# The first weight tile of the second layer is split in the gate tile's room, and the list of layer 1 gets new numbers

## The chip, the cores and the metric

The kernel runs on one core of a Trainium2 chip. The core has a TensorE for matmuls (PE in the profile; its weight loads are PEld), a VectorE (DVE), a ScalarE (ACT), a GpSimd (POOL), and a SyncE (SP) that here does nothing but issue DMAs. The metric is the device time of one execution in microseconds.

## The reference

One inference step of a small two-layer trunk with a model width of 1024, over 128 prompt tokens and 512 sample tokens. Each layer is an RMS norm, a shift and scale from the conditioning, a branch, and a gated residual. Layer 0's branch is a Conformer convolution, layer 1's a bidirectional Mamba-2 scan. What matters here is layer 1, cut to its core:

```python
def ssd_branch(h, h0_f, h0_b, w_in, w_conv, b_conv, dt_bias_f, dt_bias_b, a_log_f, a_log_b, d_skip, norm_g, w_out):
    u = h @ w_in
    z, xbc, dt_raw = jnp.split(u, [SSD_INNER, SSD_INNER + XBC_DIM], axis=-1)
    xbc = jax.nn.silu(depthwise_conv(xbc, w_conv, b_conv))
    xs, bm, cm = jnp.split(xbc, [SSD_INNER, SSD_INNER + SSD_GROUPS * D_STATE], axis=-1)
    ...
    dt_f = jax.nn.softplus(dtr_f + dt_bias_f.astype(f32))
    ...
    y_f, s_f = ssd_scan(xs, dt_f, a_f, bm, cm, h0_f)
    y_b, s_b = ssd_scan(flip(xs), flip(dt_b), a_b, flip(bm), flip(cm), h0_b)
    y = y_f + flip(y_b) + d_skip.astype(f32)[:, None] * xs.astype(f32)
    y = y.reshape(b, l, SSD_INNER) * jax.nn.silu(z.astype(f32))
    y = rms_norm(...)
    return y.astype(h.dtype) @ w_out, s_f, s_b
```

The inner width is 2048, in 32 heads of 64 that form 4 groups; the scan runs in chunks of 128 tokens (one of the prompt, four of the sample) with a state of 128.

## The kernel before

**Tiles.** Activations lie feature-major: a tile has 128 features on the partitions and all 640 tokens on the free axis, worked in two halves of 320. The input of layer 1, h, is eight such tiles. A float32 product is made of three fp32r matmuls, from a high and a low part of each operand: high by high, low by high, high by low. A weight tile of 128x1024 is loaded by an SP DMA into `wf` (two buffers), cast by ACT into its high part `wh`, and DVE subtracts that from `wf` for the low part `wl`. `wh` and `wl` are rings of three buffers each, shared by both layers.

**Layer 1's projections.** Every weight tile gives one projection tile of 48 matmuls, 320 columns wide: 8 tiles of h, 3 products, 2 halves (`project`, whose matmuls stand at L1327). There are x tiles (four per group, `x03` is group 0's last), b and c tiles (one per group) and z tiles (the gates, four per group). dt and the first two x tiles (x00, x01) are multiplied already at the end of layer 0 (L1051); they lie in `first`. After the projections of a group come the convolution over tokens, the scan of its five chunks, the norm, and the products with the output weights (`o` items, L1580, and `last_products`, L1938, for the last group), whose sums are added into x. The last group's y passes the transposes `pty` (L1750) and a sum of squares `ssp` (L1861) on PE.

**The order.** Layer 1 is written as generators that hand their steps to a list scheduler, the class `Order`. Whenever an engine's step can begin, by the list's own clocks and rings of buffers, the step of the best priority (`PRIO1`) is issued, and the tiles are taken in the order of the string `PLAN1`. So a number in these tables moves instructions on all engines. The list's clocks are set at the seam by hand: `run.clock` says when PE, ACT, DVE, POOL, SP and the DMAs are free, `run.rings.update` when the rings' buffers are, and `start(first_steps(), ...)` when dt is there. On the chip, each instruction waits for what it needs by semaphores; the list only decides the order on each engine.

**The seam.** `first_steps` empties dt's bank into `room` in two times three steps (L2133, where the list may choose ACT or DVE, and L2142, always DVE); dt's bank and the banks of x00 and x01 are the ones that layer 1's first projections take. `first_x` empties those of x00 and x01 into `up` by `evacuate` (L1357, ACT or DVE). The first weight tile's split (`split`, the case `i == 0`) is made in two halves of 512 columns, L1284 on ACT and L1271 on DVE, so that the first matmuls can begin behind the first half; all other tiles are split at L1255 and L1264.

**The gate tile.** `zs` is a room for four tiles of 640 columns that holds the gates of a group of z tiles; there is one such buffer, and nothing uses it before the first z tile of group 0.

**The end.** PLAN1 ends, before, with `x30 o10 z22 o11 x31 z23 c3 z30 z31 z32 o20 z33 o21`: group 3's last x tile is x31.

Of the kernel before, what the change touches and what calls it, by code (L numbers as in the profile page):

```python
# [8 lines left out]
F32R = mybir.dt.float32r  # L9
# [4 lines left out]
P = 128  # L14
NT = 640
# [25 lines left out]
PRIO0 = {"warm": 9, "firsts": 7, "ada_chain": 5, "modulation0": 3, "sums0": 4, "square0": 7, "first_split": -7, "conv": 3, "after_a": -5, "after_g": -7, "init": -7, "late_taps": 1, "late_adds": 3, "seam": 2, "copied": -6, "after_z": -7, "weights": 7, "split": -4, "row": 5, "square": -2, "filler": 5, "blocks": -1, "add_sums": -2, "stats": -5, "means": -3, "normalise": -4, "gate_z": 6, "late_block": -5, "residual": -3, "half_residual": -1, "root": -1, "modulation": 5, "split_h": 0, "scales": 6}  # L41
PLAN0 = "a1 z0 g2 a2 g3 a3 g4 a4 g5 a5 g6 a6 g7 a7 g8 a8 g9 a9 g10 z1 z2 a10 z3 g11 a11 g12 a12 g13 a13 g14 z4 a14 g15 z5 z6 a15 z7 z8 z9 z10 z11 z12 z13 z14 z15"
NPOOL = (12, 6, 12, 6, 12, 11, 8, 10, 2, 8, 9, 8, 12, 4, 6, 8)
PRIO1 = {"first_x": -4, "first_half": -6, "dt_way": 0, "x_way": 1, "late_weights": 0, "lead": -4, "sq_way": -3, "add_way": 6, "squares": -5, "room": -4, "roots": 4, "turn_x": -5, "gate_rows": -2, "gate_loads": 5, "residual": 5, "last_products": -3, "last_residual": -6, "final": -2, "gained_half": -7, "low": 6, "x_after": -2, "filler": 7, "decay_half": -7, "decay_state": -2, "chain0": -3, "chain1": 5, "other_y": -3, "copy_y": 2, "split_y": -5, "groups": 4, "decays": -6, "norms": 5, "gate": 7, "products1": 3, "products0": -1, "residual0": -6, "final0": -6, "w_chain": 6, "time_steps": 5, "columns": -5, "logarithm": 4, "rows_out": 7, "ends_out": 4, "weights_out": 5, "first_steps": 5, "b_after": 0, "c_after": 0, "z_after": -6, "split": -6, "add_residual": 1, "out_weights": 0, "free_bc": 2, "final1": -2, "prompt": -1, "residual1": 3, "store": -5, "final_rest": 1}
PLAN1 = "x03 x02 c0 x10 b0 z00 c1 z01 x12 x13 x33 x22 z02 x11 b1 z03 x20 c2 x23 z10 z11 z12 z13 x21 x32 b2 o00 b3 o01 z20 z21 x30 o10 z22 o11 x31 z23 c3 z30 z31 z32 o20 z33 o21"
RB1 = {"xs": 3, "st": 6, "gf": 2, "gb": 1}
WARM0 = 6
DONE0 = []
# [3 lines left out]
def trunk(ctx: ExitStack, tc: tile.TileContext, a: dict):  # L52
    nc = tc.nc
    PSUM = bass.MemoryType.PSUM
    gp = ctx.enter_context(tc.tile_pool(name="gp", bufs=1))
# [191 lines left out]
    class Order:  # L247
# [112 lines left out]
    def get(name):  # L360
        return "get", name
# [23 lines left out]
    if True:  # L385
        run = Order(PRIO0)
        post, put, start = run.post, run.put, run.start
# [56 lines left out]
        wa0, w0, x_sq, psx = {}, {}, {}, []  # L444
# [154 lines left out]
    with tc.tile_pool(name="l0", bufs=1) as lp:  # L599
# [9 lines left out]
        for i in range(3):  # L609
            t = lp.tile([P, 2, 30], F32, name=f"eb{i}")  # L610
# [309 lines left out]
        yh, yl = [None] * 16, [None] * 16  # L920
# [261 lines left out]
    lp = l1_ctx.enter_context(tc.tile_pool(name="l1", bufs=1))  # L1182
    if True:
# [7 lines left out]
        up = []  # L1191
# [37 lines left out]
        run = Order(PRIO1)  # L1229
        post, put, start = run.post, run.put, run.start  # L1230

        for name, n in (("wf", 2), ("wh", 3), ("wl", 3), ("up", 0), ("bc", 2), ("Bt", 1), ("xt", 2), ("zs", 1), ("yh", 0), ("yl", 0), ("xw", 2), ("y", 1), ("y3", 0), ("yo", 2), ("tr", 1), ("b", 3), ("gt", 1), *RB1.items()):
            run.ring(name, n)
        run.rings["mm"] = []

# [9 lines left out]
        def w_load(i, src, g=None):  # L1245
            cell = {}

            def load():
                cell["wf"] = gp.tile([P, 1024], F32, tag="wf", bufs=2, name="wf")
                nc.sync.dma_start(out=cell["wf"], in_=src)  # L1250

            def high():
                cell["wh"] = gp.tile([P, 1024], F32R, tag="wh", bufs=3, name="wh")
                if g is None:
                    S.copy(out=cell["wh"], in_=cell["wf"])  # L1255
                else:
                    for z_, sn in gained(g, cell):
                        S.activation(out=cell["wh"][:, z_], in_=cell["wf"][:, z_], func=AF.Copy, scale=sn)

            def low(e_, n=0):  # L1260
                if n == 0:
                    cell["wl"] = gp.tile([P, 1024], F32R, tag="wl", bufs=3, name="wl")
                if g is None:
                    e_.tensor_sub(out=cell["wl"], in0=cell["wf"], in1=cell["wh"].bitcast(F32))  # L1264
                else:
                    (z_, sn), = gained(g, cell)[n : n + 1]
                    e_.scalar_tensor_tensor(out=cell["wl"][:, z_], in0=cell["wf"][:, z_], scalar=sn, in1=cell["wh"][:, z_].bitcast(F32), op0=ALU.mult, op1=ALU.subtract)

            def first_half(n, t):
                z_ = slice(n * 512, n * 512 + 512)  # L1270
                t = yield either((VL, 0.69, lambda: V.tensor_sub(out=cell["wl"][:, z_], in0=cell["wf"][:, z_], in1=cell["wh"][:, z_].bitcast(F32))), (PO, 1.25, lambda: G.tensor_sub(out=cell["wl"][:, z_], in0=cell["wf"][:, z_], in1=cell["wh"][:, z_].bitcast(F32))), bias=0.5)  # L1271
                if n:
                    put("wf", t)
                W[i] = cell["wh"], cell["wl"]
                post(("w", i, "b") if n else ("w", i), t)

            def split():
                if i == 0:
                    yield get("wh")
                    yield get("wl")  # L1280
                    cell["wh"] = gp.tile([P, 1024], F32R, tag="wh", bufs=3, name="wh")
                    cell["wl"] = gp.tile([P, 1024], F32R, tag="wl", bufs=3, name="wl")
                    for n in range(2):
                        t = yield op(ACT, 0.62, lambda: S.copy(out=cell["wh"][:, n * 512 : n * 512 + 512], in_=cell["wf"][:, n * 512 : n * 512 + 512]))  # L1284
                        start(first_half(n, t), t)
                    return
                yield get("wh")
                yield op(ACT, 1.05 if g is None else 1.24, high)
                yield get("wl")
                if g is None:  # L1290
                    t = yield either((VL, 1.22, lambda: low(V)), (PO, 2.41, lambda: low(G)), bias=PRIO1["low"])
                else:
                    yield op(VL, 0.77, lambda: low(V))
                    t = yield op(VL, 0.77, lambda: low(V, 1))
                put("wf", t)
                W[i] = cell["wh"], cell["wl"]
# [861 lines left out]

        with tc.manual_schedule():
            S.activation(out=an, in_=c("alog"), func=AF.Exp)  # L2160
# [146 lines left out]
```

## Time and profile before

| what | value |
|---|---|
| median of 3 runs | 1057.93 us (1057.34 to 1058.88) |
| profiled execution | 1056.0 us, its span 1054.2 us |
| granted TensorE clock | 0.997 |
| PE busy | 98% of the span, 7497 instructions |
| layer 1's first projection matmul | at 544.95 us |
| last x tile of group 3 ends on PE | at about 915.5 us |
| last matmul | begins just before 1046 us |

A row of the timeline gives the start in us, the busy time, engine, line, operation, and what is written from what; in brackets stands how long the engine had been idle and what released it. A row of a window gives the stretch and the busy time of PE, PEld, DVE, ACT and POOL. PE's busy time counts pipelined matmuls, so an idle gap is read from the times of the rows' starts.

### The profile page before, as it was taken

The page shows a single profiled execution, that of the slowest core. Times are in us where ns is not written, and L with a number is a line of the kernel's source. Part 1 is how long each engine was busy: PE and PEld are TensorE (multiplying, and loading weights), DVE is VectorE, ACT ScalarE, POOL GpSimd, SP SyncE. Part 2 cuts the span into 40 slices and gives each one's busy share as a digit, 9 for nine tenths or more (in the row PEclk, how much of TensorE's full clock was granted, in tenths as well). Part 3 has the DMA queues.
Part 4 walks back from the last instruction along what each step waited for, and adds up shares of the span by engine and source line. Part 5 has one row for each costly group of instructions (what it writes and reads, how often), then busy time and mean ns, then how long its engine had stood idle before and what let it go on. Part 6 is the DMA issues. An engine that isn't in the chain of part 4 may idle for free.

```text
span 1054.2 us, 19251 instructions
## 1 busy us (share of the span) xinstructions
PE 1030.5 (98%) x7497; PEld 945.9 (90%) x7497; DVE 814.8 (77%) x1219; ACT 670.5 (64%) x1115; POOL 475.8 (45%) x472
## 2 busy tenths in 40 slices
PE   6999999999999999999999999999999999999996
PEld 4999999999999999999989998899888878897865
DVE  3599999998997679202589858889598777896797
ACT  6468788778687578433477755588665455474534
POOL 0029989978596511111000046414544555426551
PEclk9999999999999999999999999999999999999998
DMA  9597888788856666777112252333424334323423
GB/s 355 205 269 196 195 210 202 180 212 215 186 123 143 136 143 149 150 155 165 61 58 85 83 160 91 110 115 107 131 83 120 117 101 130 113 98 104 126 81 100
DMA packets 64363, 151.82 MB, mean 144 GB/s; under 512 B 9472, under 2 KB 22416, under 8 KB 64272
## 3 DMA queue, kind: packets, MB, share of 16 engines
q1 hardware_dynamic: 54048, 118.87, 35.9%
q0 software_dynamic: 8640, 30.94, 17.4%
q8 instruction: 59, 0.97, 0.4%
q10 hardware_dynamic: 1584, 0.79, 0.3%
q14 instruction: 32, 0.26, 0.1%
HBM read 145.45 MB, written 5.12 MB: 143 GB/s over the span
## 4 chain that ended last, share of the span: by engine, by line
PE 86%; DVE 7%; ACT 2%; DMA 2%; issue 2%; SPq 0%; DVEq 0%; ACTq 0%
PE xs L1327 9%; PE pz L1327 8%; PE o L1580 6%; PE pst L1660 3%; PE po L1723 2%; PE C L1327 2%; PE B L1327 2%; PE py L1791 2%; PE o__4964 L158 1%; PE o__5264 L158 1%; PE o__5273 L158 1%; PE o__5251 L158 1%; PE o__5244 L158 1%; PE o__4954 L158 1%; PE xs L1051 1%
## 5 line engine op out<-in xcount | busy, mean ns | idle before, releaser
L815 DVE SCALAR_TENSOR_TENSOR cva<-v,cst,cva 128x550 f32<-128x550 f32 (+12 forms) x346 | 270.2, 823 | 11.2 <-ACT cva L807 6.1
L887 POOL TENSOR_TENSOR cv<-cv,tp 128x490 f32<-128x490 f32 (+5 forms) x134 | 172.5, 1287 | 8.5
L846 ACT ACTIVATE tp<-v,cst 128x490 f32<-128x490 f32 (+5 forms) x134 | 92.3, 717 | 35.9 <-POOL cv L887 35.5
L425 ACT CAST wh<-wf 128x1024 fp32r<-128x1024 f32 x63 | 66.0, 1047 | 63.9 <-PE o__5273 L158 30.0
L1327 PE MATMUL pz<-h_hi,wh 128*128 128x320 f32 x256 | 87.2, 341 | 0.0
L1327 PE MATMUL pz<-h_hi,wl 128*128 128x320 f32 x256 | 79.1, 309 | 0.0
L1327 PE MATMUL pz<-h_lo,wh 128*128 128x320 f32 x256 | 79.0, 309 | 0.0
L1327 PE MATMUL xs<-h_hi,wh 128*128 128x320 f32 x224 | 77.0, 344 | 1.9 <-DVE room L2142 1.9
L1327 PE MATMUL xs<-h_hi,wl 128*128 128x320 f32 x224 | 69.4, 310 | 0.1
L1327 PE MATMUL xs<-h_lo,wh 128*128 128x320 f32 x224 | 69.1, 309 | 0.0
L1373 DVE SCALAR_TENSOR_TENSOR xs<-up,cst,xs 128x642 f32<-128x642 f32 x64 | 64.8, 1013 | 3.2 <-ACT xs L1371 1.9
L1729 POOL TENSOR_TENSOR y<-y,yo 128x512 f32<-128x512 f32 x32 | 45.4, 1421 | 41.4 <-DVE yo L1727 41.4
L1255 ACT CAST wh<-wf 128x1024 fp32r<-128x1024 f32 x37 | 38.6, 1046 | 38.3 <-PE pz L1327 10.6
L435 ACT ACTIVATE wl<-wh 128x1024 fp32r<-128x1024 f32 x58 | 61.5, 1061 | 1.7
L436 POOL DMA_DIRECT2D wl<-w_in x43 | 37.4, 869 | 55.0 <-ACT wl L435 52.0
L1597 POOL TENSOR_TENSOR gb<-gb,cols 128x512 f32<-128x512 f32 x20 | 25.8, 1290 | 79.3 <-DMA gb<-acb 79.3
L1559 POOL TENSOR_TENSOR x<-x,tmp 128x512 f32<-128x512 f32 x30 | 45.5, 1520 | 34.5 <-DVE tmp L1555 34.4
L1264 DVE TENSOR_TENSOR wl<-wf,wh 128x1024 fp32r<-128x1024 f32 x37 | 48.5, 1315 | 14.6 <-ACT wh L1255 12.8
L1603 ACT ACTIVATE gf<-gf,cols 128x128 f32<-128x128 f32 x160 | 50.6, 391 | 10.4 <-DVE gf L1599 10.0
L436 POOL DMA_DIRECT2D wl<-w_out x15 | 12.9, 862 | 90.5 <-ACT wl L435 90.5
L1580 PE MATMUL o<-wh,yh 128*128 128x512 f32 x120 | 52.4, 436 | 0.4 <-DVE tmp L1555 0.4
L1327 PEld LDWEIGHTS pz<-h_hi,wh 128*128 128x128 f32 x256 | 48.2, 188 | 3.5 <-issue 3.4
(849 smaller groups left out, 3536.1 us busy)
## 6 DMA issues: line engine op xcount, KB each, us to landing
wf<-w_in SPq DMA_DIRECT2D x48, 512.0 KB, 3.7
wl<-w_in POOLq DMA_DIRECT2D x43, 512.0 KB, 6.4
wa<-w_ada SPq DMA_DIRECT2D x64, 256.0 KB, 5.9
wf<-w_out SPq DMA_DIRECT2D x32, 512.0 KB, 3.6
wf<-w_xbc SPq DMA_DIRECT2D x24, 512.0 KB, 3.6
gf<-acf SPq DMA_DIRECT2D x40, 256.0 KB, 4.0
wa<-w_ada SPq DMA_DIRECT2D x16, 512.0 KB, 10.8
wf<-w_z SPq DMA_DIRECT2D x16, 512.0 KB, 3.6
```

What stands on the lines that cost most here:

```text
L158: T.matmul(ps[:, b, at : at + t1 - t0], lhsT=w, rhs=h[:, t0:t1], start=first and n == 0, stop=last and n == 2)
L425: t = yield op(ACT, 1.05, lambda: S.copy(out=wh, in_=wf))
L435: yield op(ACT, 1.06, lambda: S.activation(out=wl, in_=wh.bitcast(F32), func=AF.Copy, scale=-1.0))
L436: t = yield op(PD, 0.7, lambda: G.dma_start(out=wl, in_=src, accum_op=ALU.add))
L815: t = yield op(VE, 0.24 + 0.01 * (hi - lo), lambda: V.scalar_tensor_tensor(out=rows64(accs[i], lo, hi), in0=rows64(vs[i], lo + d, hi + d), ...
L846: t = yield op(ACT, 0.72, lambda: S.activation(out=tp[:, :, 0 : hi - lo], in_=rows64(vs[i], lo + d, hi + d), func=AF.Copy, scale=w_dw(i, t ...
L887: t = yield op(PO, 1.3 + 0.019 * (hi - lo - 49), lambda: G.tensor_add(out=rows64(cv[i], lo, hi), in0=rows64(cv[i], lo, hi), in1=sgs["tp", ...
L1264: e_.tensor_sub(out=cell["wl"], in0=cell["wf"], in1=cell["wh"].bitcast(F32))
L1327: T.matmul(ps[:, b, at_ : at_ + t1 - t0], lhsT=w_, rhs=t_[:, t0:t1], start=k == 0 and n == 0, stop=k == nk - 1 and n == 2)
L1373: t = yield op(VL, 0.97, lambda: V.scalar_tensor_tensor(out=acc, in0=u[:, d : d + PW], scalar=c("w_c", j * 5 + d), in1=acc, op0=ALU.mult, ...
L1580: T.matmul(ps, lhsT=t_, rhs=w_, start=k == 0 and n == 0, stop=k == 3 and n == 2)
L1603: t = yield op(ACT, 0.39, lambda: S.activation(out=gv[:, h_, :], in_=gv[:, h_, :], func=AF.Exp, bias=cols1[ch][:, o8 + h_ : o8 + h_ + 1]), ...
```

## The change

Three things change, and all other code stays.

1. The first weight tile (item 0 of the list) takes the room of `zs`, as a tile called `w0`: its first 1024 columns are the high part, the next 1024 the low. It takes no buffer of the rings `wh` and `wl`; when its projection has been multiplied, `w_free` gives `zs` back.
2. The list's times at the seam: ACT's and DVE's clocks go from −2.0 to −3.0, the free times of `wh` and `wl` from −1.8, −0.9, 0.0 to −0.8, −0.4, 0.0, the start of `first_steps` from −1.8 to −0.8, of `first_x(0)` from −0.9 to −0.4.
3. All of `PRIO1` and `PLAN1` is new.

```diff
-PLAN1 = "x03 x02 c0 x10 b0 z00 c1 z01 x12 x13 x33 x22 z02 x11 b1 z03 x20 c2 x23 z10 z11 z12 z13 x21 x32 b2 o00 b3 o01 z20 z21 x30 o10 z22 o11 x31 z23 c3 z30 z31 z32 o20 z33 o21"
+PLAN1 = "b0 x12 z00 c0 x03 x02 x10 x33 z01 z02 x23 x13 z03 c1 x11 b1 z10 z11 z12 x20 x31 o00 x21 x22 z13 o01 z20 c2 b2 z21 x30 z22 z23 b3 o10 c3 o11 x32 z30 z31 z32 o20 z33 o21"
...
-        for name, n in (("wf", 2), ("wh", 3), ("wl", 3), ("up", 0), ("bc", 2), ("Bt", 1), ("xt", 2), ("zs", 1), ...
+        for name, n in (("wf", 2), ("wh", 3), ("wl", 3), ("up", 0), ("bc", 2), ("Bt", 1), ("xt", 2), ("zs", 0), ...
...
                 if i == 0:
-                    yield get("wh")
-                    yield get("wl")
-                    cell["wh"] = gp.tile([P, 1024], F32R, tag="wh", bufs=3, name="wh")
-                    cell["wl"] = gp.tile([P, 1024], F32R, tag="wl", bufs=3, name="wl")
+                    yield get("zs")
+                    room_ = lp.tile([P, 4, NT], F32R, tag="zs", bufs=1, name="w0").rearrange("p a b -> p (a b)")
+                    cell["wh"], cell["wl"] = room_[:, 0:1024], room_[:, 1024:2048]
...
         def w_free(i, t):
+            if i == 0:
+                put("zs", t)
+                return
             put("wh", t)
             put("wl", t)
...
-            run.clock = [0.0, -2.0, -2.0, -2.0, -9.0, -9.0]
+            run.clock = [0.0, -3.0, -3.0, -2.0, -9.0, -9.0]
...
-            run.rings.update(wf=[-9.0, -9.0], wh=[-1.8, -0.9, 0.0], wl=[-1.8, -0.9, 0.0])
+            run.rings.update(zs=[-9.0], wf=[-9.0, -9.0], wh=[-0.8, -0.4, 0.0], wl=[-0.8, -0.4, 0.0])
...
-            start(first_steps(), -1.8)
-            start(first_x(0), -0.9)
+            start(first_steps(), -0.8)
+            start(first_x(0), -0.4)
```

Line numbers behind `split` move by two at most: L1284 becomes L1283, L1327 becomes L1329, L1357 becomes L1359. In the new code the L2133 form is ACT's step for dt, and DVE's two are L2135 and L2144. The order of layer 0's instructions is the same on every engine.

ACT at the seam, from the first instruction of layer 1 (`an`) on. `up_6270` and `up_6274` are the copies of x00 and x01, `dt` is dt's bank; the names in brackets are the semaphores that the instruction waits for (DMAHW5 is the load of the weights). Before:

```order
L2160 ACTIVATE an<-cst 128x1 [waits DVE_49]
L1284 CAST wh<-wf 128x512 [waits DMAHW5_49,PE_49]
L1284 CAST wh<-wf 128x512
L1255 CAST wh<-wf 128x1024 [waits DMAHW6_49,PE_49]
L1357 COPY up_6270<-xs 128x128 [waits PE_49]
L1357 COPY up_6274<-xs 128x64
L1357 COPY up_6274<-xs 128x64 [waits PE_49]
L1357 COPY up_6270<-xs 128x512
```

and in the changed kernel:

```order
L2162 ACTIVATE an<-cst 128x1 [waits DVE_49]
L1283 CAST w_6300<-wf 128x512 [waits DMAHW5_49]
L1283 CAST w_6300<-wf 128x512
L1255 CAST wh<-wf 128x1024 [waits DMAHW6_49,PE_49]
L1359 COPY up_6270<-xs 128x128 [waits PE_49]
L2133 ACTIVATE room_6286<-dt,cst 32x128 [waits DVE_49,Pool_49]
L1359 COPY up_6270<-xs 128x512
L2133 ACTIVATE room_6286<-dt,cst 32x256
```

The first two casts no longer wait for PE, and two steps of dt have come over from DVE, one of them ahead of the second copy of x00.

DVE at the same place, from its first step of dt on; before:

```order
L2133 TENSOR_SCALAR room_6286<-dt,cst 32x128 [waits DMASW0_49,DMASW1_49,DVE_49,DMAHW6_49,PE_49,Pool_49]
L2133 TENSOR_SCALAR room_6286<-dt,cst 32x256
L2142 TENSOR_SCALAR room_6286<-dt,cst 32x256
L2133 TENSOR_SCALAR room_6286<-dt,cst 32x128
L2133 TENSOR_SCALAR room_6286<-dt,cst 32x256
L2142 TENSOR_SCALAR room_6286<-dt,cst 32x256
L1271 TENSOR_TENSOR wl<-wf,wh 128x512 [waits DMAHW5_49,Activation_49]
L1271 TENSOR_TENSOR wl<-wf,wh 128x512 [waits Activation_49]
L1264 TENSOR_TENSOR wl<-wf,wh 128x1024 [waits DMAHW6_49,PE_49,Activation_49]
```

and in the changed kernel:

```order
L2135 TENSOR_SCALAR room_6286<-dt,cst 32x128 [waits DMASW0_49,DMASW1_49,DVE_49,DMAHW6_49,PE_49,Pool_49]
L2135 TENSOR_SCALAR room_6286<-dt,cst 32x256
L2144 TENSOR_SCALAR room_6286<-dt,cst 32x256
L1271 TENSOR_TENSOR w_6300<-wf,w_6300 128x512 [waits DMAHW5_49,Activation_49]
L1271 TENSOR_TENSOR w_6300<-wf,w_6300 128x512 [waits Activation_49]
L1264 TENSOR_TENSOR wl<-wf,wh 128x1024 [waits DMAHW6_49,Activation_49]
L2144 TENSOR_SCALAR room_6286<-dt,cst 32x256 [waits Activation_49]
```

The split of the first tile now stands behind three steps of dt instead of six, and dt's last step behind the split of the second tile.

PE, from the last matmul of layer 0 on; before:

```order
L1051 MATMUL xs<-h_hi,wh 128x320
L1051 MATMUL xs<-h_lo,wh 128x320
L1051 MATMUL xs<-h_hi,wl 128x320
L1327 MATMUL xs<-h_hi,wh 128x320 [waits DVE_49,PE_49,Activation_49]
L1327 MATMUL xs<-h_lo,wh 128x320
L1327 MATMUL xs<-h_hi,wl 128x320 [waits DVE_49]
```

and in the changed kernel, where item 0 is b0:

```order
L1051 MATMUL xs<-h_hi,wh 128x320
L1051 MATMUL xs<-h_lo,wh 128x320
L1051 MATMUL xs<-h_hi,wl 128x320
L1329 MATMUL B<-h_hi,w_6300 128x320 [waits PE_49,Activation_49]
L1329 MATMUL B<-h_lo,w_6300 128x320
L1329 MATMUL B<-h_hi,w_6300 128x320 [waits DVE_49]
```

The first projection's bank is no longer dt's, which DVE frees, but x00's, which ACT's second copy frees; the third matmul waits for the low half's split as before.

More of the change, by code (lines that the diff above doesn't have):

```diff
@@ L43 @@
 NPOOL = (12, 6, 12, 6, 12, 11, 8, 10, 2, 8, 9, 8, 12, 4, 6, 8)
-PRIO1 = {"first_x": -4, "first_half": -6, "dt_way": 0, "x_way": 1, "late_weights": 0, "lead": -4, "sq_way": -3, "add_way": 6, "squares": -5, "room": -4, "roots": 4, "turn_x": -5, "gate_rows": -2, "gate_loads": 5, "residual": 5, "last_products": -3, "last_residual": -6, "final": -2, "gained_half": -7, "low": 6, "x_after": -2, "filler": 7, "decay_half": -7, "decay_state": -2, "chain0": -3, "chain1": 5, "other_y": -3, "copy_y": 2, "split_y": -5, "groups": 4, "decays": -6, "norms": 5, "gate": 7, "products1": 3, "products0": -1, "residual0": -6, "final0": -6, "w_chain": 6, "time_steps": 5, "columns": -5, "logarithm": 4, "rows_out": 7, "ends_out": 4, "weights_out": 5, "first_steps": 5, "b_after": 0, "c_after": 0, "z_after": -6, "split": -6, "add_residual": 1, "out_weights": 0, "free_bc": 2, "final1": -2, "prompt": -1, "residual1": 3, "store": -5, "final_rest": 1}
-PLAN1 = "x03 x02 c0 x10 b0 z00 c1 z01 x12 x13 x33 x22 z02 x11 b1 z03 x20 c2 x23 z10 z11 z12 z13 x21 x32 b2 o00 b3 o01 z20 z21 x30 o10 z22 o11 x31 z23 c3 z30 z31 z32 o20 z33 o21"
+PRIO1 = {"first_x": 0, "first_half": 6, "dt_way": 1, "x_way": 3, "late_weights": -6, "lead": -4, "sq_way": 3, "add_way": 7, "squares": -5, "room": -4, "roots": -3, "turn_x": 3, "gate_rows": -3, "gate_loads": 6, "residual": 2, "last_products": 2, "last_residual": -1, "final": 3, "gained_half": -3, "low": 4, "x_after": -2, "filler": 6, "decay_half": -1, "decay_state": 4, "chain0": -3, "chain1": 5, "other_y": -3, "copy_y": 0, "split_y": -3, "groups": 1, "decays": 6, "norms": -1, "gate": 5, "products1": -4, "products0": 6, "residual0": 7, "final0": 6, "w_chain": -1, "time_steps": 3, "columns": 3, "logarithm": -7, "rows_out": 3, "ends_out": 5, "weights_out": 0, "first_steps": -2, "b_after": -2, "c_after": 7, "z_after": 6, "split": -6, "add_residual": -5, "out_weights": 3, "free_bc": 2, "final1": 4, "prompt": -3, "residual1": -7, "store": -2, "final_rest": -2}
+PLAN1 = "b0 x12 z00 c0 x03 x02 x10 x33 z01 z02 x23 x13 z03 c1 x11 b1 z10 z11 z12 x20 x31 o00 x21 x22 z13 o01 z20 c2 b2 z21 x30 z22 z23 b3 o10 c3 o11 x32 z30 z31 z32 o20 z33 o21"
 RB1 = {"xs": 3, "st": 6, "gf": 2, "gb": 1}
@@ L1230, in trunk @@
         post, put, start = run.post, run.put, run.start
-        for name, n in (("wf", 2), ("wh", 3), ("wl", 3), ("up", 0), ("bc", 2), ("Bt", 1), ("xt", 2), ("zs", 1), ("yh", 0), ("yl", 0), ("xw", 2), ("y", 1), ("y3", 0), ("yo", 2), ("tr", 1), ("b", 3), ("gt", 1), *RB1.items()):
+        for name, n in (("wf", 2), ("wh", 3), ("wl", 3), ("up", 0), ("bc", 2), ("Bt", 1), ("xt", 2), ("zs", 0), ("yh", 0), ("yl", 0), ("xw", 2), ("y", 1), ("y3", 0), ("yo", 2), ("tr", 1), ("b", 3), ("gt", 1), *RB1.items()):
             run.ring(name, n)
```

## Prediction

> **What bounds the kernel now.** I read the page's busy line and its chain first, then PE's waits, then PE's idle time by stage, then the seam between the layers instruction by instruction.
>
> ```profile
> PE 1030.5 (98%) x7497; PEld 945.9 (90%) x7497; DVE 814.8 (77%) x1219; ACT 670.5 (64%) x1115; POOL 475.8 (45%) x472
> PE 86%; DVE 7%; ACT 2%; DMA 2%; issue 2%; SPq 0%; DVEq 0%; ACTq 0%
> ```
>
> The first line says that TensorE is busy for all but 23.7 us of a span of 1054.2 us; the second that the chain which ends last runs through PE for 86% of it. So this kernel is a queue of matmuls, and a reordering can win only what PE waits for, plus what comes behind its last matmul. PE's waits by cause:
>
> ```profile
> PE rps L200 <- ACT rms_sq L507: 7.1, 1, 7.1
> PE xs L1327 <- DVE room L2142: 1.9, 1, 1.9
> PE ssp L1861 <- DVE ysq L1856: 1.5, 3, 0.8
> PE ada L544 <- DMA wa<-w_ada: 0.9, 1, 0.9
> ```
>
> The longest, 7.1 us for the first squares, lies at the start of layer 0, whose order is unchanged. The second is the wait of layer 1's first projection tile: the seam, which the change is about. The rest is small change. By stage, layer 1 behind the seam, up to the end of the last x tile of group 3 (about 915.5 us) and from there to the last matmul:
>
> ```profile
> 545.20:915.50 370.30, 369.23 (x2365) 327.09 (x2365) 296.77 (x409) 231.53 (x423) 153.16 (x118) 1.00 0.37 113
> 915.50:1046.30 130.80, 126.86 (x714) 103.98 (x712) 112.44 (x195) 71.82 (x145) 58.16 (x45) 1.00 0.34 101
> ```
>
> The columns are the stretch, its length, and the busy time of PE, weight loads, DVE, ACT and POOL. PE idles for 370.30 − 369.23 = **1.07 us** in the middle and for 130.80 − 126.86 = **3.94 us** in the tail, at a granted clock of 1.00. In the tail DVE is busy for 112.44 of 130.80 us.
>
> The seam itself:
>
> ```profile
> 539.73 0.20 ACT L2160 ACTIVATE an<-cst 128x1 f32<-128x1 f32 x1
> 542.10 1.14 ACT L1284 CAST wh<-wf 128x512 fp32r<-128x512 f32 x2 [2.17 <-PE dt L1051]
> 542.31 0.73 DVE L2133 TENSOR_SCALAR room<-dt,cst 32x128 f32<-32x128 f32 x2 [3.25 <-PE dt L1051]
> ...
> 542.78 0.31 PE L1051 MATMUL xs<-h_hi,wl 128*128 128x320 f32 x1
> 543.05 0.48 DVE L2142 TENSOR_SCALAR room<-dt,cst 32x256 f32<-32x256 f32 x1
> 543.15 1.04 ACT L1255 CAST wh<-wf 128x1024 fp32r<-128x1024 f32 x1
> 543.54 0.75 DVE L2133 TENSOR_SCALAR room<-dt,cst 32x128 f32<-32x128 f32 x2
> 544.09 1.51 ACT L1357 COPY up<-xs 128x128 f32<-128x128 f32 x6
> 544.30 0.49 DVE L2142 TENSOR_SCALAR room<-dt,cst 32x256 f32<-32x256 f32 x1
> 544.83 1.30 DVE L1271 TENSOR_TENSOR wl<-wf,wh 128x512 fp32r<-128x512 f32 x2
> ...
> 544.95 0.39 PE L1327 MATMUL xs<-h_hi,wh 128*128 128x320 f32 x1 [1.85 <-DVE room L2142]
> ...
> 545.17 0.31 PE L1327 MATMUL xs<-h_lo,wh 128*128 128x320 f32 x1
> ...
> 545.58 0.41 PE L1327 MATMUL xs<-h_hi,wl 128*128 128x320 f32 x1
> ```
>
> PE's last layer-0 matmul starts at 542.78. ACT idled for 2.17 us until the dt projection had given up a weight buffer, and only then cast the first tile. DVE emptied the dt bank in six steps until 544.79; PE's first tile needs that bank and starts at 544.95; its third matmul needs half of DVE's split behind those steps and starts at 545.58. Matmuls of this form follow each other every 0.147 us:
>
> ```profile
> 915.56 0.31 PE L1327 MATMUL pz<-h_hi,wh 128*128 128x320 f32 x1
> 915.70 0.31 PE L1327 MATMUL pz<-h_lo,wh 128*128 128x320 f32 x1
> ```
>
> At that pace the third would have started at 542.78 + 3 × 0.147 = 543.22, so the seam costs 545.58 − 543.22 = **2.36 us**. Nothing done here can bring more than that.
>
> **The change part by part.** All sums stand against the profiled execution (span 1054.2, its own time 1056.0 us); that is 1.9 below the median of the three runs, and I carry the difference over to 1057.93.
>
> *The split in the gate tile's room.* The same two casts and two subtractions stay; only where they write, and so what they wait for, changes. The weights are there long before:
>
> ```profile
> 514.10 4.80 SPq L1250 DMA_DIRECT2D wf<-w_xbc  x2
> L1357 ACT COPY up<-xs 128x128 f32<-128x128 f32 x2 | 0.5, 262 | 0.0
> L1357 ACT COPY up<-xs 128x512 f32<-128x512 f32 x2 | 1.2, 606 | 0.0
> ```
>
> The load was issued at 514.10, some 25 us ahead. So the casts start when ACT is free, 539.93, and end at 539.93 + 1.14 = 541.07, in the 2.17 us in which ACT idled: their price is nothing, and that idle time is the cover. If the room were not free they would stand where they stand now.
>
> Behind them, walked by hand: ACT's cast of the second tile still waits for dt's weight buffer, 542.10 to 543.14. The 128x128 copy takes 0.26, to 543.40. ACT has now been given two of the six dt steps. The first of them waits behind DVE's third, which ends at 542.31 + 0.73 + 0.48, about 543.53. No row shows such a step on ACT: from below the 128x1 row (0.20), from above the 128x512 copy (0.606); I take 0.26, the nearest (a copy of the same 128 columns), to about 543.85. The 128x512 copy, which is queued behind it on ACT, ends at 544.45, and that copy is what frees the bank that PE's first tile now takes. PE starts 0.1 later, 544.55. DVE meanwhile goes straight from 543.53 to the split, so its first half (0.65) is ready at 544.2 and no longer waited for; the third matmul starts at 544.55 + 0.29 = 544.84. **Seam: 545.58 − 544.84 = 0.74 gained.** Bounds: 1.2 gained if the step costs nothing and waits for nothing (copy from 543.40 to 544.0; DVE's half at 544.2 then sets the third matmul, at 544.4); 0.4 lost if the casts stay behind 542.10 (then casts, second cast, copy, step and copy follow each other to 545.5, and the third matmul comes at 545.95). What is late next is the copy on ACT, so 1.6 of the 2.36 us stay.
>
> *The new order.* It holds the same tiles, so PE's work is equal; what changes is waiting. Three places:
>
> 1. The time-step chain. b0 and not x03 comes first, and the column transposes stand about 15 us earlier in PE's order.
>
> ```profile
> 600.10 0.49 PE L2097 MATMUL pt<-cst,room 128*128 128x128 f32 x3
> ```
>
> They ran at 600.10. With 15 us less ahead of them, and the seam's 0.74, PE reaches them at about 584. The chain on DVE that they wait for holds 40.8 us of steps from 542.31 on, so 583.1 plus whatever DVE idles on the way. That is a dead heat: 0 to 1.0 us of new wait; I take **+0.2**, since a slip has to exceed 0.8 first.
>
> 2. The middle (1.07 us idle now). ACT loses 8 table loads, each 1283 ns: 10.3 us of ACT.
>
> ```profile
> L1603 ACT ACT_TABLE_LOAD x17 | 21.8, 1283 | 7.0 <-DVE gf L1599 6.7
> ```
>
> But ACT is busy for 231.53 of 370.30 us there, and only small waits end on it. So I give this little: **−0.3** between −1.07 (all waits go) and +1.7 (as many new ones, of the size of the seam's present wait).
>
> 3. The tail. Before, x31 is group 3's last x and z23, c3 stand behind it; now x32 is, and both stand ahead. Two tiles of 48 × 0.147 = 7.04 us, with small differences 15.1 us, of PE work less stand behind the point from which group 3's scan can run. DVE's rows behind it, counted at the means of their groups, shrink by 13.2 us. Slack of DVE against PE: 130.8 − 112.4 = 18.4 before, (130.8 − 15.1) − (112.4 − 13.2) = 16.5 now. DVE's share hardly moves (112.4/130.8 = 86%, 99.2/115.7 = 86%), but the 3.94 us of waits fall in its dense stretch:
>
> ```profile
> 1010.00:1020.00 10.00, 9.52 (x43) 6.79 (x41) 9.76 (x16) 4.12 (x9) 4.96 (x4) 1.00 0.57 171
> 1020.00:1030.00 10.00, 8.50 (x36) 6.65 (x37) 9.83 (x19) 3.64 (x10) 2.94 (x2) 1.00 0.01 5
> 1020.76 0.35 PE L1861 MATMUL ssp<-ones,ysq 128*128 128x1 f32 x2 [0.79 <-DVE ysq L1856]
> ```
>
> DVE is 98% busy there and PE waits for it. Counting, for each PE tile that waits for DVE, the DVE work left less the PE work left, the worst point is +5.8 us before and +6.0 after: **+0.2**, between −1 and +3.5 (the rival below).
>
> *The end.* After the last matmul come DVE's multiply and addition, ACT's square and the store. The last piece is now a 256-wide one:
>
> ```profile
> 1046.23 0.75 DVE L1953 SCALAR_TENSOR_TENSOR tmp<-o,rs,gt 128x512 f32<-128x512 f32 x1 [0.38 <-PE o L1938]
> 1047.02 0.69 DVE L1963 TENSOR_TENSOR x<-x,tmp 128x512 f32<-128x512 f32 x1
> ...
> 1039.74 0.48 DVE L1953 SCALAR_TENSOR_TENSOR tmp<-o,rs,gt 128x256 f32<-128x256 f32 x1
> 1040.58 0.99 DVE L1961 TENSOR_TENSOR x<-x,tmp 128x256 f32<-128x256 f32 x2
> ```
>
> That saves 0.27 + 0.19 on DVE and about 0.2 on ACT, but DVE has a step of 0.75 of the piece before queued ahead. I take **0**, between −0.7 and 0.
>
> Sum: −0.74 + 0.2 − 0.3 + 0.2 + 0 = **−0.64**, so 1057.93 − 0.64 = **1057.3 us**.
>
> [...]
>
> ```profile
> 960.00:970.00 10.00, 10.00 (x51) 6.67 (x51) 5.92 (x7) 3.39 (x7) 8.20 (x8) 1.00 0.28 86
> ```
>
> This stretch has PE at 10.00, no wait, and loads at 6.67: 51 wide matmuls simply need fewer loads. An order can't win there, and my sum keeps to the waits.
>
> **The rivals.**
>
> *Faster.* PE's small waits go with the seam's. For it: there are 1.07 + 3.94 = 5.0 us of them behind the seam, and ACT and DVE have room on the whole. Against it: nothing in the change takes DVE work out of the tail. Seam 0.74, middle 1.07 and a third of the tail 1.3: 3.1, **1054.8 us**; everything would give 1052.2. It decides where PE's idle in the tail falls below about 2.5.
>
> *Slower.* Group 3 starts later and DVE paces the tail. The last transposes of y stand 93 matmuls from the end of PE's order, and stood 108 before. For a 512-wide matmul:
>
> ```profile
> 1041.13 0.40 PE L1938 MATMUL o<-wh,yh 128*128 128x512 f32 x1
> 1041.37 0.39 PE L1938 MATMUL o<-wh,yl 128*128 128x512 f32 x1
> ```
>
> that is 15 × 0.235 = 3.5 us less cover for DVE. If DVE stays at 9.8 of 10 from there on, PE waits for all of it: 3.5 − 0.74 = +2.8, **1060.7 us**. It decides once the y of the last chunk reaches PE over 1.5 us late. For it: the windows of 1010 to 1030. Against it: the count above, +6.0 against +5.8. POOL could bring it about:
>
> ```profile
> 987.60 1.49 POOL L1738 TENSOR_TENSOR y<-xt,co 128x512 f32<-128x512 f32 x1
> 997.59 1.04 POOL L1738 TENSOR_TENSOR y<-xt,co 128x512 f32<-128x512 f32 x1 [1.64 <-DVE co L1777]
> ```
>
> the same addition took 1.49 us beside DVE's split and 1.04 otherwise; three of them ahead of a transpose make 3 × 0.45 = 1.35. [...]
>
> *No effect at the seam.* The casts still wait for something: +0.4 there, **1058.3 us**.
>
> **How the numbers follow.** A measurement of this kernel tells about 0.2%, 2.1 us, from no change. Forecast, between 1055.8 and 1060.0: 0.47. No effect: 0.04, also within. Faster: 0.31, as the order's 5.0 us of other waits are more than the 1.4 it needs besides the seam. Slower: 0.18, as it needs 2.1 + 0.74 of new waits. Hence faster 0.31, same 0.51, slower 0.18. The range reaches from 1053.6, where most of the tail's waits have gone too, to 1060.2, short of the whole of the slower rival: about 0.1 is left out on each side.
>
> **What would show it.** At the seam, ACT's two casts at about 540, and PE's first L1329 matmul at about 544.55 with a wait on ACT; a wait on DVE, or a start after 545, would make that step wrong. In the middle, PE's idle time near 1 us and no wait over 1 us at the column transposes (a long one there is step 1 wrong). In the tail, about 4 us of idle; below 2.5 is the faster rival, above 6 the slower one. Any change ahead of 538 us would be wrong altogether: that order is the same.

## The result and the profile after

The changed kernel takes **1062.97 us** (median of 4 runs, 1062.67 to 1065.11) against 1058.06 for the kernel before: a ratio of 1.0059, 95% interval 1.0047 to 1.0071. It is about 5 us slower, where I had forecast a gain of 0.64 us and put the chance of slower at 0.18. The profiled execution has a span of 1060.9 us, 6.7 more than before. Lines behind `split` are higher by two. One execution further down ran at a mean clock of 0.558 (1686.1 us; the record has the clock of the kernel's own core and nothing of the rest of the chip) and is compared with nothing; all others had 0.993 or more.

The page's busy line and its chain of work, and PE's waits:

```profile
PE 1032.6 (97%) x7497; PEld 947.3 (89%) x7497; DVE 815.2 (77%) x1215; ACT 661.3 (62%) x1110; POOL 480.1 (45%) x473
PE 88%; DVE 7%; DMA 2%; issue 1%; ACT 1%; SPq 0%; DVEq 0%; ACTq 0%
...
PE ssp L1863 <- DVE ysq L1858: 6.3, 5, 2.6
PE B L1329 <- ACT up L1359: 1.5, 1, 1.5
PE xs L1329 <- DVE tmp L1557: 1.3, 1, 1.3
PE pty L1752 <- POOL y L1731: 0.7, 2, 0.4
```

DVE's work is the same to 0.4 us, and ACT has 9 us less. What has grown is one kind of wait: PE at the sums of squares (ssp), for DVE, 6.3 us where it was 1.5. By stage, with the cut where group 3's last x tile ends, now at 936.4:

```profile
545.20:936.40 391.20, 385.30 (x2474) 342.22 (x2473) 314.23 (x434) 235.41 (x441) 155.14 (x118) 1.00 0.36 110
936.40:1052.30 115.90, 111.97 (x604) 89.47 (x602) 94.89 (x164) 57.98 (x122) 59.94 (x46) 0.99 0.33 98
```

PE idles for 5.90 us in the middle (1.07 before) and for 3.93 in the tail (3.94 before). **The loss is in the middle.** The last column but two, the granted clock, is 0.99 in the tail; that is a second, smaller loss, shown below.

The seam went almost as walked (here and below, rows that lie between the ones shown are left out):

```profile
539.92 1.13 ACT L1283 CAST w<-wf 128x512 fp32r<-128x512 f32 x2
543.71 0.36 ACT L2133 ACTIVATE room<-dt,cst 32x128 f32<-32x128 f32 x1 [0.31 <-DVE room L2144]
544.08 0.59 ACT L1359 COPY up<-xs 128x512 f32<-128x512 f32 x1
544.72 0.41 PE L1329 MATMUL B<-h_hi,w 128*128 128x320 f32 x1 [1.54 <-ACT up L1359]
545.11 0.46 PE L1329 MATMUL B<-h_hi,w 128*128 128x320 f32 x2
```

Layer 0's last matmul starts at 542.87 here, so the third of layer 1 comes 2.24 us behind it, where it was 2.80: 0.56 won.

Two waits of the middle, one of them the longest, show what happened there:

```profile
671.47 0.41 DVE L1857 TENSOR_TENSOR ysq<-ysq 128x256 f32<-128x256 f32 x1
671.86 1.04 POOL L1740 TENSOR_TENSOR y<-xt,co 128x512 f32<-128x512 f32 x1 [0.86 <-PE pty L1752]
671.91 1.13 DVE L1858 TENSOR_TENSOR ysq<-ysq 128x128 f32<-128x128 f32 x1
673.19 0.35 PE L1863 MATMUL ssp<-ones,ysq 128*128 128x1 f32 x2 [1.05 <-DVE ysq L1858]
...
808.25 0.75 DVE L1557 SCALAR_TENSOR_TENSOR tmp<-o,rs,gt 128x512 f32<-128x512 f32 x1
808.91 3.45 DVE L1264 TENSOR_TENSOR wl<-wf,wh 128x1024 fp32r<-128x1024 f32 x2
809.08 2.21 POOL L1561 TENSOR_TENSOR x<-x,tmp 128x512 f32<-128x512 f32 x1 [2.27 <-DVE tmp L1557]
812.29 0.41 DVE L1857 TENSOR_TENSOR ysq<-ysq 128x256 f32<-128x256 f32 x1
812.73 0.29 DVE L1858 TENSOR_TENSOR ysq<-ysq 128x128 f32<-128x128 f32 x1
813.17 0.35 PE L1863 MATMUL ssp<-ones,ysq 128*128 128x1 f32 x2 [1.85 <-DVE ysq L1858]
```

In the kernel before, one split with no POOL row beside it reads:

```profile
546.04 1.22 DVE L1264 TENSOR_TENSOR wl<-wf,wh 128x1024 fp32r<-128x1024 f32 x1
```

At 808.91 DVE's two splits take 3.45 us, where two plain ones would take 2.44; POOL's addition beside them takes 2.21 us, where the fastest of its 30 takes 1.27. Both take longer side by side, DVE reaches the ysq additions a microsecond late, and PE stands. At 671.91 the collision hits the ysq addition itself: beside POOL's L1740 it takes 1.13 us, at 812.73 it takes 0.29. That the rest of the waits in the middle came in the same way is not read off single rows; the runs with shortened POOL additions below show it.

The kernel's list writes down a time for each step that it issues. The start in the profile, less 542.9, less the list's time, is how late DVE runs against its plan (mean over 20 us of list time):

```
list time of DVE's steps, us   40    100   120   140   240   260   380   440   460   500
before: late by               1.2   0.9   1.0   1.0   0.6   1.8   1.8   2.2   2.9   3.4
after: late by                0.2   0.8   2.9   3.8   3.9   5.5   6.4   7.0   9.2  11.0
```

By the list's own times the new order ends 1.1 us sooner (502.8 against 503.9). On the chip it falls behind in steps: 2 us around 120, 1.6 around 260, 1.3 before 380, and 4 from 440 on (the last lies in the tail). The list does know of collisions: in the class `Order` POOL's steps and most of DVE's steps with two inputs in SBUF (the on-chip memory where the tiles lie) share a clock, `port`, so they are planned one after the other. But only the order on each engine reaches the chip. There 110 of these 344 DVE steps run beside a POOL step for more than 0.25 us, and in the kernel before 109 of 346.

### The profile page after: what moved, and what is told of

Read it like the earlier page. It is cut to its first block, busy times and chain, and to the rows that moved or that the text cites. A ratio compares the mean times of both kernels' runs of the same rounds, so it can differ in the third digit from the quotient of the medians.

```text
span 1060.9 us, 19223 instructions
## 1 busy us (share of the span) xinstructions
PE 1032.6 (97%) x7497; PEld 947.3 (89%) x7497; DVE 815.2 (77%) x1215; ACT 661.3 (62%) x1110; POOL 480.1 (45%) x473
## 4 chain that ended last, share of the span: by engine, by line
PE 88%; DVE 7%; DMA 2%; issue 1%; ACT 1%; SPq 0%; DVEq 0%; ACTq 0%
PE pz L1329 9%; PE xs L1329 8%; PE o L1582 7%; PE B L1329 3%; PE pst L1662 2%; PE o L1940 2%; PE C L1329 2%; PE po L1725 2%; PE py L1793 2%; PE o__4964 L158 1%; PE o__5273 L158 1%; PE o__5244 L158 1%; PE o__4954 L158 1%; PE o__5251 L158 1%; PE o__5264 L158 1%
## 5 line engine op out<-in xcount | busy, mean ns | idle before, releaser
L1329 PE MATMUL pz<-h_hi,wh 128*128 128x320 f32 x256 | 84.4, 330 | 0.0
L1329 PE MATMUL pz<-h_hi,wl 128*128 128x320 f32 x256 | 79.1, 309 | 0.0
L1329 PE MATMUL pz<-h_lo,wh 128*128 128x320 f32 x256 | 79.1, 309 | 0.0
L1329 PE MATMUL xs<-h_hi,wh 128*128 128x320 f32 x224 | 76.9, 343 | 1.3 <-DVE tmp L1557 1.3
L1264 DVE TENSOR_TENSOR wl<-wf,wh 128x1024 fp32r<-128x1024 f32 x37 | 51.2, 1389 | 24.7 <-ACT wh L1255 24.5
L1329 PE MATMUL xs<-h_hi,wl 128*128 128x320 f32 x224 | 69.2, 309 | 0.0
L1329 PE MATMUL xs<-h_lo,wh 128*128 128x320 f32 x224 | 69.1, 309 | 0.0
L1329 PEld LDWEIGHTS pz<-h_hi,wh 128*128 128x128 f32 x256 | 48.2, 188 | 2.4 <-issue 2.3
```

The costliest lines, as they stand in the source:

```text
L1329: T.matmul(ps[:, b, at_ : at_ + t1 - t0], lhsT=w_, rhs=t_[:, t0:t1], start=k == 0 and n == 0, stop=k == nk - 1 and n == 2)
```

## The experiments

**How the order was held.** A changed number in `PRIO1` changes hundreds of rows: the new `PLAN1` can't be combined with the old `PRIO1` without upsetting the whole order. So in six experiments the list's choices were replaced by a written list of them, which gives every engine the order of the kernel it was taken from, and single rows were then moved. (Moving the sums in the first experiment also shifted some of DVE's rows and one of ACT's; in the others only the moved rows differ.)

### The sums of squares later on PE

```diff
 # written order of the changed kernel, PE
-ssp (group 0 to 2, each chunk)
 product (3 matmuls) x1 to x5
+ssp (group 0 to 2, each chunk)
```

> The changed kernel with its own order written out row by row, in which one kind of row is moved: the 15 sums of squares (ssp) of groups 0 to 2 stand six products (6 x 3 matmuls, 2.6 us of PE) later on PE. Before the move PE waits at four of them for DVE's ysq additions: 1.2, 0.7, 1.9 and 0.4 us, 4.2 in all. Theory A (the new order asks for them before DVE can have them, and PE has other work at hand): all four waits go, 1063.0 - 4.2 = 1058.8 us. Theory B (DVE itself sets the pace there): PE waits at the next row that needs DVE, and the time stays within 1 us of 1063.0.

Three executions took 1063.4, 1067.4 and 1068.1 us. The profile is that of the execution at a mean clock of 0.558, in which PE waits at no sum of squares, so the same kernel ran once more.

> The kernel of the first experiment once more, for a profile at the full clock: its profile was taken while the whole chip was throttled (a mean clock of 0.558), so it shows no waits that can be read. Its three other runs took 1063.4 to 1068.1 us, so theory A's 1058.8 has not come. Theory B (DVE sets the pace): the four ssp waits (4.2 us) are gone or smaller, and waits of about the same sum stand at the next rows that need DVE, the profiled execution within 2 us of 1062.7. Theory C (the moved sums delay the group's root, and with it the residual that frees the o tile's bank): the new waits stand at o tiles of L1612 and name DVE's tmp.

1065.49 us (1064.95 to 1066.03), 2.5 us above the changed kernel: more than theory B's 1 us allows, too. PE's waits in this profile:

```profile
PE ssp L1893 <- DVE ysq L1888: 5.7, 5, 2.5
...
PE pcb L1803 <- DVE xt L1786: 1.3, 1, 1.3
PE po L1755 <- ACT xt L1793: 1.3, 2, 0.7
...
545.20:939.00 393.80, 387.42 (x2471) 343.40 (x2469) 312.56 (x431) 234.50 (x438) 155.45 (x118) 1.00 0.36 109
```

The traces show a smaller move than the expectations say: the sums stand 3 to 15 matmuls later on PE, not 18. At 673 it was six matmuls. The waits there shrank from 1.05 and 0.57 us to 0.16 and 0.40, and new ones at pcb (1.32) and po (0.65) took their place. At the longest wait it was only three matmuls, and it shrank from 1.85 to 1.41 us, by just the 0.44 us that three matmuls take. The middle idles for 393.80 − 387.42 = 6.4 us instead of 5.9. Theory C is out (no wait at an o tile of L1612 for DVE's tmp came with the move). Theory A's gain did not come, but at 813 the move was too short to test it. Where it was long enough, the wait moved on to the next row that needs DVE: this speaks for **DVE setting the pace there**. Which of DVE's and POOL's work makes it late is tested below.

### One sum of squares later in the tail

```diff
 # written order of the changed kernel, PE
-ssp (group 3, chunk 0)
 last_products x2
+ssp (group 3, chunk 0)
```

> The changed kernel with its own order written out, and one row moved: the first ssp that waits in the tail (2.55 us at 1019.4, after which PE's clock is granted at 0.50 for about 3.5 us) stands four product groups of last_products (2.8 us of PE) later. Theory A (only its place is wrong): wait and slow clock both go, 2.55 + 1.4 = 3.9, 1059.1 us, and no window shows a clock of 0.50. Theory B (DVE paces the tail): the clock's 1.4 us go or not, PE then waits at the py products for DVE's gf, and at most 1.5 us are won, 1061.5 us.

1063.82 us (1063.36 to 1064.04), nothing won. In the trace the sum stands six matmuls later (two groups, 1.4 us), not four groups. The wait of 2.55 us became a chain of smaller ones, from `o` for a weight's low half (0.65) to `py` (0.77), and the tail idles for 115.70 − 111.71 = 4.0 us as before:

```profile
937.50:1053.20 115.70, 111.71 (x604) 88.06 (x603) 95.78 (x164) 57.91 (x122) 60.62 (x46) 1.00 0.34 99
```

The stretch at half clock is gone from the tail (1.00), yet in this execution one stands in the middle, behind a wait of 1.04 us at 673.57. Theory B again, as far as this shorter move tests it.

### The rows of the end

```diff
 # written order of the changed kernel, DVE; in the second kernel ACT's store too
-L1996 x<-x,fin,fgb   (chunk before the last)
 last piece: L1955, L1963
+L1996 x<-x,fin,fgb   (chunk before the last)
```

> The changed kernel with its own order written out, and one DVE row of the end moved: the multiplication L1996 that took 1.83 us at 1051.81, in the same moment as POOL's L1987, where others of its kind take 0.75, stands behind the last piece's two steps. If that collision lies on the path that ends last, 1.0 to 1.3 us are won (about 1061.8 us). If the end is set elsewhere, nothing (1063.0).

1062.93 us: nothing. In the changed kernel these rows end the program:

```profile
1051.81 1.83 DVE L1996 SCALAR_TENSOR_TENSOR x<-x,fin,fgb 128x512 f32<-128x512 f32 x1
1051.81 1.28 POOL L1987 TENSOR_TENSOR x<-x,fgb 128x512 f32<-128x512 f32 x1 [3.98 <-ACT tmp L1966]
1053.67 0.38 ACTq L1998 DMA_DIRECT2D o_y<-x  x1
1054.64 0.42 ACT L1966 ACTIVATE tmp<-x 128x256 f32<-128x256 f32 x1 [1.89 <-DVE x L1963]
```

and with DVE's row moved:

```profile
1053.20 0.74 DVE L2026 SCALAR_TENSOR_TENSOR x<-x,fin,fgb 128x512 f32<-128x512 f32 x1
1053.97 0.38 ACTq L2028 DMA_DIRECT2D o_y<-x  x1
1054.40 0.42 ACT L1996 ACTIVATE tmp<-x 128x256 f32<-128x256 f32 x1 [1.81 <-DVE x L2026]
```

The collision is gone (0.74 instead of 1.83), but ACT's queue still holds the store of that row ahead of its last square. So the store was moved as well:

> The changed kernel's own order with rows of the end moved: DVE's multiplication and, this time, the store behind it on ACT's queue too, now behind ACT's last square. In the third experiment the DVE row alone was moved, and ACT's last square still began at 1054.40 behind the store's issue, which waits for that row. If this queueing is what holds up the end, the stretch from the last matmul to the end of the span falls from 8.6 to 7.6 us or less, 1.0 us; if not, it stays 8.6.

1062.70 us (1061.67 to 1063.77). From the last matmul's end to the span's end it is 1060.87 − 1052.84 = 8.0 us, as in the kernel before (8.0), where the changed kernel has 8.6. With the DVE row alone moved it was still 8.6. So the collision and the queueing behind it cost 0.6 here, not 1.0, and the median can't tell that from nothing.

### The old order with the new seam

The room and ACT's two steps of dt, with everything behind the seam in the order of before:

```diff
-                    cell["wh"] = gp.tile([P, 1024], F32R, tag="wh", bufs=3, name="wh")
-                    cell["wl"] = gp.tile([P, 1024], F32R, tag="wl", bufs=3, name="wl")
+                    room_ = lp.tile([P, 4, NT], F32R, tag="zs", bufs=1, name="w0").rearrange("p a b -> p (a b)")
+                    cell["wh"], cell["wl"] = room_[:, 0:1024], room_[:, 1024:2048]
...
 # written order of the kernel before, its first 22 rows taken from the changed kernel
```

> The order of the kernel before, written out row by row, with the seam of the changed kernel: the first weight tile in the gate tile's room, and two of dt's steps on ACT; from the first projection on every engine's order is that of before. If the seam's part is independent of the order, PE's third matmul starts about 2.24 us after the last one of layer 0 instead of 2.80, and 0.5 us are won: 1057.5 us. If the room or ACT's two steps cost something later, it is 1058.1 or more.

**1055.13 us** (1054.89 to 1056.08, 10 runs) against 1057.65 of the kernel before beside it (13 runs): a ratio of 0.9981, interval 0.9972 to 0.9990. This version beats both kernels.

```profile
541.94 0.31 PE L1080 MATMUL xs<-h_hi,wl 128*128 128x320 f32 x1
543.79 0.41 PE L1359 MATMUL xs<-h_hi,w 128*128 128x320 f32 x1 [1.54 <-ACT up L1389]
544.04 0.31 PE L1359 MATMUL xs<-h_lo,w 128*128 128x320 f32 x1
544.18 0.46 PE L1359 MATMUL xs<-h_hi,w 128*128 128x320 f32 x2
```

544.18 − 541.94 = 2.24 us, exactly the changed kernel's seam: its gain doesn't depend on the order. The profiled executions differ by 0.9 us (1055.13 against 1056.0), the medians by 2.5, where I had expected 0.5; the further 1.6 is taken up under the clock, below.

### POOL's additions cut

DVE is late on the new order. Is it the work of DVE itself, or POOL's? In two kernels, called light here, POOL's two costliest additions of layer 1 work on a part of their columns; the rest of the output is left out.

```diff
-G.tensor_add(out=x_, in0=x_, in1=as_part(tmp, ch))
+G.tensor_add(out=x_[:, 0:1], in0=x_[:, 0:1], in1=as_part(tmp, ch)[:, 0:1])
...
-G.tensor_add(out=y, in0=y, in1=yo)
+G.tensor_add(out=y[:, 0:64], in0=y[:, 0:64], in1=yo[:, 0:64])
```

> The changed kernel, same order on every engine, with two of POOL's additions in layer 1 cut to a part: x plus the residual (L1561) works on 128 of 512 columns and y plus yo (L1731) on 64, so those parts of the output are left out. That takes some 55 of POOL's longest rows out of DVE's way. Theory D (DVE's and POOL's collisions make DVE late on this order): PE's idle time behind the seam falls from about 13 us to 6 or less, and this kernel ends within 1 us of the old order with the same cut. Theory E (DVE has too much plain work before those points, whatever POOL does): PE's waits at ssp stay at 5 us or more, and this kernel stays 4 us or more above the old order with the same cut.

> The kernel before with the same two additions cut in the same way (L1559 and L1729), its order unchanged; the same parts of the output are left out. It is the partner of the run with the new order. It should win little, since its waits behind the seam are 5 us in all: 1 to 3 us below the kernel before, by both theories.

1053.00 us (1052.23 to 1053.97) with the new order and 1052.05 (1050.40 to 1052.73) with the old: the gap of 5 us has shrunk to 0.95. The old order won 4.8 us against the kernel before beside it (1056.89), more than the 1 to 3 expected. The middle of the new order, and below it that of the old:

```profile
545.20:928.50 383.30, 383.29 (x2470) 341.87 (x2469) 292.78 (x434) 234.92 (x439) 111.57 (x118) 1.00 0.37 113
...
545.20:915.70 370.50, 370.23 (x2366) 328.69 (x2365) 283.28 (x410) 231.76 (x423) 113.52 (x118) 1.00 0.38 113
```

PE's idle time in the middle of the new order went from 5.90 us to 0.01. DVE has exactly the same instructions, yet is busy for 292.8 us there instead of 314.2: over 21 us of DVE's "work" in the middle were stretch, and went with the cut columns of POOL's additions. Behind the seam as a whole PE's idle time fell from 9.8 us (the expectation's 13 is too much) to 4.1, nearly all of it in the tail. Theory D.

But shorter additions also deliver sooner. So in two more kernels, called filled, they were given back their length, by memsets that read nothing:

```diff
+G.memset(tmp[:, 128:512], 0.0); G.memset(tmp[:, 128:512], 0.0)
 G.tensor_add(out=x_[:, 0:1], in0=x_[:, 0:1], in1=as_part(tmp, ch)[:, 0:1])
...
+G.memset(yo[:, 64:512], 0.0); G.memset(yo[:, 64:512], 0.0)
 G.tensor_add(out=y[:, 0:64], in0=y[:, 0:64], in1=yo[:, 0:64])
```

> The new order with the same two POOL additions cut as in the light kernel, but ahead of each stand two memsets of the part of tmp (384 columns) or yo (448) that the cut addition doesn't read, so that POOL is busy about as long as in the changed kernel (a memset of 384 columns took 0.42 us, so 0.84 or 0.98 more) and its results come as late, while in that time it only writes. The same parts of the output are left out. Theory D1 (it is POOL's reading beside DVE that makes DVE late): about the time of the light kernel, 1053 to 1055 us, DVE's L1264 pair at about 806 near its plain 2.4 to 2.6 us. Theory D2 (it is only that POOL's results come late): back to 1060 us or more.

> The old order with the same cut and the same memsets. Theory D1: like the old order's light kernel, 1052 to 1054 us, so the two orders stay within 1.5 us of each other. Theory D2: 1056 to 1058 us, 4 us or more below the new order.

1053.09 us (1052.99 to 1053.64) and 1052.14 (1051.46 to 1053.38): as without the memsets. The page's busy line of the new order with memsets, its middle, and the place that stood at 808.91 before:

```profile
PE 1027.9 (98%) x7497; PEld 945.1 (90%) x7497; DVE 788.5 (75%) x1215; ACT 661.4 (63%) x1110; POOL 467.3 (44%) x597
...
545.20:929.10 383.90, 383.47 (x2470) 341.72 (x2470) 294.12 (x434) 234.96 (x439) 146.14 (x206) 1.00 0.38 113
...
803.51 2.62 DVE L1264 TENSOR_TENSOR wl<-wf,wh 128x1024 fp32r<-128x1024 f32 x2
803.66 0.90 POOL L1561 MEMSET tmp<- 128x384 f32 x2 [1.46 <-DVE tmp L1557]
804.52 0.53 POOL L1561 TENSOR_TENSOR x<-x,tmp 128x128 f32<-128x128 f32 x1
```

POOL is busy for 467.3 us, nearly the 480.1 of the changed kernel, and the middle idles for 0.43 us. The two splits take 2.62 us, where they took 3.45 beside the whole addition; POOL's two memsets and what is left of its addition take 0.90 + 0.53 = 1.43 us, no less than a plain addition (1.27). So in these runs neither POOL's busy time beside DVE nor the later result brought the waits back. What the memsets lack against the columns that they stand for is the **reading** of two tiles: a memset's row has no input. Theory D1, with one limit: the runs don't tell the reads from the arithmetic that goes with them.

### The kernel before once more

> The kernel before, unchanged, for a second profile. Its runs beside the experiments had a mean clock of 0.998 in 1053.6 to 1054.7 us of span and of 0.996 in 1055.4 to 1056.6; the old order with the new seam had 0.998 or 0.999 in all ten. Theory F (the stall at the seam is long enough that in most executions PE's clock drops behind it): a profile of 0.996 has a stretch at half the clock right behind 545 us, and that stretch makes up the 1.5 to 2 us. Theory G (the drop is elsewhere, at the start or in the tail): the seam's stretch has a clock of 1.00 there too.

1055.99 us at a mean clock of 0.998; every window of 2 us up to 1048, behind its last matmul, has a granted clock of 1.00. This profile decides neither theory. The profile of the light kernel on the old order, which has the old seam, bears on F; it is read in the last section.

## Why the prediction was wrong

- **What bounds the kernel**: right. PE is the queue, and the change won and lost only in PE's waits, behind its last matmul, and in its clock.
- **The split in the gate tile's room**: right in mechanism, a little large. 0.74 forecast, 0.56 measured, twice. ACT's step of dt took 0.36 where I took 0.26 from the nearest copy, and PE started 1.85 us behind layer 0's last matmul rather than 1.77; its third matmul came another 0.39 later rather than 0.29.
- **The time-step chain**: forecast +0.2, measured 0. The first transposes stand at 584.37, where I had put them (584), and PE waits for none of them.
- **The middle: this is the step that failed.** I wrote "−0.3 between −1.07 and +1.7"; measured is 5.90 − 1.07 = +4.83. I read the middle off the waits that were there, all small, and off ACT's relief. Neither says what a new order makes of DVE: with two-input rows of DVE and additions of POOL laid differently, DVE comes late at places where PE waits for it, and the light and the filled kernels show that with most columns of POOL's two costliest additions left out nearly all of the 5.9 us go (0.01 and 0.43 are left). I had the rows for it (1.49 against 1.04 us), but placed the collision in the tail. And my upper bound, "as many new ones, of the size of the seam's present wait", was an analogy, not a price: DVE was 80% busy in the middle before (296.8 of 370.3 us), and a stretch of about 1 us per collision (3.45 against 2.44, 1.83 against 0.75) can fall ahead of any of 15 sums of squares.
- **The tail**: +0.2 forecast, 0.0 in idle time (3.93 against 3.94). Moving one sum of it by six matmuls left the idle time as it was (4.0), which speaks for DVE pacing it, as the forecast's rival had it; but the idle time was the same before. What came on top is the clock: about 1.4 us in the profiled execution.
- **The end**: 0 forecast, bounds −0.7 to 0, measured +0.6. The shorter last piece is there, but the chain that ends last runs through a DVE row that POOL stretched from 0.75 to 1.83 us, ahead of the last piece's steps; with that row moved, the store behind it held up ACT's queue instead. I had counted instructions behind the last matmul, not what is queued ahead of them.
- **The sum**: −0.56 + 0 + 4.83 + 1.4 + 0.6 = 6.3 of the 6.7 us between the two spans.
- **The rivals**: the slower one had the right sign and over half the size (+2.8 forecast against +4.9), and named POOL's collision as a possible agent, but in the wrong place, the tail.

What the experiments don't settle: which of the new numbers makes the order collide more at the tight places. The numbers work only together, and DVE's rows are stretched by about as much in total as before (61 against 59 us behind the seam, each row counted by what it takes above the fastest tenth of its form). So it is hardly more collisions. That it is where they fall is the reading that is left; no run shows it by itself.

## What to carry to other kernels

When a list of costs chooses a new order, its gain of 1 us by its own clocks is worth nothing if the chip doesn't keep the list's times: this list planned POOL's steps and DVE's two-input steps apart, and on the chip they met (110 of 344 for more than 0.25 us). Look in the trace for rows of one form with two durations, and ask at each place where the bounding engine will wait how much in hand the helping engine has. A change with two parts is to be measured in two parts: here the seam alone, on the old order, was worth having. And a wait that moves on to the next row when its matmul is moved says that the engine waited for sets the pace. Before that is concluded, count in the trace how far the row moved.

## What the runs showed of the hardware

In these traces the granted clock of PE dropped behind some short stalls. In the changed kernel, behind the wait of 2.55 us in the tail:

```profile
1019.41 0.35 PE L1863 MATMUL ssp<-ones,ysq 128*128 128x1 f32 x2 [2.55 <-DVE ysq L1858]
1020.30 0.63 PE L1940 MATMUL o<-wl,yh 128*128 128x512 f32 x1
1020.73 0.63 PE L1940 MATMUL o<-wh,yh 128*128 128x512 f32 x1
...
1021.00:1022.00 1.00, 1.00 (x3) 0.73 (x3) 1.00 (x3) 0.00 (x0) 0.58 (x1) 0.50 0.16 53
```

The granted clock (third column from the end) is 0.50, and a matmul starts every 0.43 us instead of 0.23 (at 1016.00 and 1016.23, ahead of the wait), for seven of them: 7 × 0.195 = 1.4 us. The waits of 1.05 us at 673.19 and of 1.85 at 813.17 left the clock at 1.00 in that execution. In the kernel with the moved tail row a wait of 1.04 us at 673.57 was followed by a clock of 0.50 from 674.16 to 677.58; in the one with all sums moved, a stall of 1.41 us between 813 and 815 by the same from 816.52 to 819.93. So in these executions a stall of one to two and a half microseconds did or didn't cost some 1.4 us more.

In all six profiles that have such a stretch ahead of the last matmul it lasts 3.4 us (3.41 in the changed kernel, from 1020.01 to 1023.42). Idle time alone doesn't decide it. In the kernel with the moved tail row PE was idle for 1.41 of the 3.41 us ahead of 674.16, and the clock fell; it was idle for 1.56 us between 812 and 814 and for 0.29 in the next two, and the clock stayed at 1.00. What decides is open.

The kernel before, in 29 runs beside the experiments, has a mean clock of 0.998 in 1053.6 to 1055.0 us of span, 0.997 in 1054.0 to 1055.1, and 0.996 in 1055.1 to 1056.6. As an estimate from the stretches above, 3.41 us at half the clock cost up to 1.7 us and 0.0016 of the mean, so about one such stretch lies between 0.998 and 0.996. The old order with the new seam showed 0.998 or 0.999 in ten of ten. The obvious reading is that its shorter stall at the seam (1.54 us against 1.85) avoids a stretch, and one profile supports it: the light kernel on the old order, which has the old seam with the same wait of 1.85 us, ran at a clock of 0.50 from 545.69 to 549.11, right behind that wait. Its page agrees: the matmuls of the x tiles (L1327), the first of which stands there, are busy for 217.6 us, where the filled kernel on the same order has 215.6, and those of the gates for 245.4 in both. It is one of four profiles with the old seam; none of the eight readable ones with the new seam has a stretch there. That the unchanged kernel's runs at 0.996 have it too is not shown: both of its profiles have the full clock behind the seam.
